# Router logits by feature blocks inside the last two column groups of an output projection, with a hand-written order and contiguous float16 parts

## The chip, the cores and the metric

The kernel runs on one core of a Trainium2 chip. Its metric is device time in microseconds, from one launch. The engines are TensorE (matrix products, transposes), VectorE, ScalarE, GpSimd (POOL) and SyncE (SP, which issues the loads). Each has its own queue and takes its instructions in the order of that queue; engines wait for each other by semaphores.

## The reference, cut to what matters

One block of a hybrid model for 512 tokens with 1024 features, in float32: gated mixing, cross attention, then a mixture of 32 experts in 4 groups, each added to the residual, and a last norm. The part that is touched is the end of the cross attention and the router:

```python
x = x + o.reshape(B, S, D) @ w_xo            # the residual, 512 x 1024
h = _rmsnorm(x, g_moe)                       # x * rsqrt(mean(x*x) + eps) * g
g_logits = h @ w_rg + b_rg                   # 4 groups
g_idx = argmax(g_logits)
e_logits = h @ w_re + b_re                   # 4 x 8 experts, those of the group g_idx count
top_v, top_i = top_k(e_sel, 2)               # two experts a token, softmax weights
for e in range(32):                          # only the chosen tokens have weight
    y += combine[:, e] * ((silu(h @ w_gate[e]) * (h @ w_up[e])) @ w_down[e])
```

Since the norm is one number per token and one gain per feature, the logits can be had from the raw residual: the gain goes into the router's weights beforehand, and the token's number is multiplied in afterwards.

## The kernel before, in words

Tokens stand in four blocks of 128 on the partitions; X1 (X2 inside `moe`) is the residual, block by block. Float32 products of the projections are made of three products of split operands (`mm3`, lines 98 to 101): the operand's high part, which ScalarE writes (line 121 for weights), and its low part, which VectorE writes (line 122).

`w_xo` is multiplied in four groups of 256 columns. The groups 0 and 1 are started inside the last head of the attention. Groups 2 and 3 follow: group 2 by halves of the features (`half`, 48 products each, 12 a block), group 3 block by block (`of_block`, 24 products), so that block 0 of the residual is ready first. The adds into the residual are line 522. `load_w` keeps three raw buffers and two pairs of split buffers; the numbers in `wx` give one load of this stage an extra raw buffer, and one an extra pair.

The router of a block is in `moe`: `turn` transposes the block's residual (line 755, eight transposes; columns are taken with a step of 8, as expert weights are laid out with eight consecutive features on a partition), ScalarE evacuates the first four (758) and VectorE the other four (760); line 762 squares and sums; the power -0.5 runs on POOL (95). `parts` scales the block and splits it into two float16 parts, the high one on ScalarE (771), the low one on VectorE (772). Both read the residual in order and write feature q*8+j to place j*128+q. `logits` is eight products of 40 columns (780). `choose` (786 to 810), for two blocks at once, picks group and experts with small VectorE instructions; `place` (812 to 831) counts, by products with a triangle of ones, which slot of its expert a token takes, and writes the selections of the first pair of experts (737, 738). `first` (875) gathers the first pair's tokens: products of the float16 parts with the selections. `numbers` (835 to 865) prepares each slot's token number (products of line 851) and the exponentials of the weights, and ends with a small Silu that brings its table in.

The experts go by pairs of two: gate and up products (1033, 64 a pair), transposes (1046), down products (1057), gathering for the next pair (1008, its copy 1010), combination (1083 to 1085). Weight pieces of 1 MB come in a ring of some fourteen buffers (922, 927) from a list in order of use; ten of the buffers have one size, and the router's transposes take one of those ten until its logits are done.

The order of work: a planner orders each engine's instructions by its own estimate of when they are ready, earlier-written work first. In a `manual_schedule` region the named engines keep the written order among the region's instructions; a region inside another adds its engines to those of the outer one, and the outer engines' order runs through it. Before, only TensorE has a written order: that of ROUT for the router, and that of the pairs for the experts. In ROUT a `w` is a block of group 3 (`w34` stands for four of its steps), T a turn, L logits, X parts, C choose, K place, G first, N numbers.

Of the kernel before, what the change touches and what calls it, by code (L numbers as in the profile page):

```python
# [9 lines left out]
F32 = mybir.dt.float32  # L10
# [10 lines left out]
P = 128  # L21
# [21 lines left out]
ROUT = "w0 w1 T0 w2 T1 w34 L0 T2 w3 L1 T3 C0 X0 X1 L2 L3 C1 K0 X2 X3 K1 G0 G1 N0 N1"  # L43
# [11 lines left out]
def emit(ctx, tc, a):  # L55
# [27 lines left out]
    colsv = consts.tile([P, 32], F32, name="colsv")  # L83
# [23 lines left out]
    def load_w(src, k0, nk, c0, n):  # L107
# [7 lines left out]
        if i == 3:  # L115
# [9 lines left out]
    def drain(g):  # L125
        for _ in g:
            pass
# [423 lines left out]
    rt_ = router_consts(ctx, nc, a, left, colsv[:, 24:32])  # L551
# [108 lines left out]
    rw = resid_rows(a["w_xo"], oth, otl, 2)  # L660
    drain(rw.half(0))
    drain(rw.half(4))
    rw.done()
    rw = resid_rows(a["w_xo"], oth, otl, 3)
    rw.loads()
    experts.load(NAHEAD)
    with tc.manual_schedule(engines={mybir.EngineType.PE}):
        fill = [rw.of_block(tb) for tb in range(NB)]

        def go(g, n=99):  # L670
            for _ in range(n):
                if next(g, "end") == "end":
                    return
        for w in ROUT.split():
            if w[0] == "w":
                go(fill[int(w[1])], int(w[2:] or 99))
            elif w[0] == "N":
                with tc.issue_after(router[-1].after_v):
                    router["N"](int(w[1]))
            else:  # L680
                router[w[0]](int(w[1]))
# [4 lines left out]
def router_consts(ctx, nc, a, left, gcol):  # L686
# [4 lines left out]
    c.gsc = rc.tile([P, KB], F32, name="gsc")  # L691
    V.tensor_scalar(c.gsc, gcol, 1.0 / XS, None, op0=OP.mult)
    c.wr = rc.tile([P, KB, NR], F32, name="wr")
    SP.dma_start(c.wr, a["w_r"])
    V.tensor_mul(c.wr, c.wr, c.gsc[:, :, None].to_broadcast([P, KB, NR]))
# [32 lines left out]
def moe(ctx, tc, a, X2, dram, small, acc, pss, pso, left, right, ident, rpow, wp, c, mraw):  # L728
# [16 lines left out]
    sq, lgs, m8s, ids = {}, {}, {}, {}  # L745

    def turn(tb):

        if not tTs:
            tTs.append(mraw.tile([P, 2, KB, P], F32, name="rsc", tag="mw", bufs=NRAW))  # L750
        tT = tTs[0][:, tb % 2]
        for j0 in range(0, KB, 4):
            pt = pss()
            for j in range(4):
                TE.transpose(pt[:, j * P:(j + 1) * P], X2[tb][:, j0 + j::KB], ident)
            ptv = pt.rearrange("p (j t) -> p j t", j=4)
            if j0 == 0:
                S.activation(tT[:, j0:j0 + 4], ptv, AF.Copy)
            else:
                V.tensor_copy(tT[:, j0:j0 + 4], ptv)  # L760
# [504 lines left out]
```

## Time and profile before

| | |
|---|---|
| median of three runs | 1316.55 us (1315.34 to 1319.72) |
| profiled execution | 1316.15 us, of it the span from first to last instruction 1314.4 us |
| TensorE busy | 1254.6 us, 95% of the span, mean granted clock 0.978 |
| VectorE, ScalarE, POOL busy | 561.8, 363.5, 128.9 us |
| loads | 278.45 MB, mean 212 GB/s, some 415 GB/s in the last third |

Times count from the first instruction. The projections with `w_xo` end, and the router runs, between some 730 and 815; the experts fill the rest. The granted clock is 1.0 where TensorE runs at 2.4 GHz and 0.5 at 1.2 GHz. A group of instructions has its line, engine and operation, output and input with their shapes, and its count. Busy time is a sum over instructions that may overlap.

### The profile page before, as it was taken

What the parts mean: (1) busy time and instruction counts of PE and PEld (TensorE: products, weight loads), DVE (VectorE), ACT (ScalarE), POOL (GpSimd) and SP (SyncE); (2) the same over time, 40 slices, a digit from 0 to 9 for tenths busy, and PEclk for the clock granted to TensorE, in tenths of its full rate; (3) what the DMA queues carried; (4) which work ended last, traced back from release to release, by engine and by line L of the source; (5) the groups of instructions that cost most, each with busy time, mean ns of one, the idle gap of its engine ahead of it and who ended that gap; (6) DMA issues with size and microseconds to landing.
All of it is one profiled execution on the core that took longest, in us unless ns stands there. A gap on an engine that the chain in (4) does not pass through costs nothing.

```text
span 1314.4 us, 18626 instructions
## 1 busy us (share of the span) xinstructions
PE 1254.6 (95%) x7606; PEld 903.1 (69%) x7606; DVE 561.8 (43%) x1050; ACT 363.5 (28%) x616; POOL 128.9 (10%) x250
## 2 busy tenths in 40 slices
PE   6999999999999999999999966999999999999996
PEld 5898998888888877899888965444444444444443
DVE  5346365234565645447455446132232322222225
ACT  5335343223344433336333253010000000000102
POOL 0002010000001100001000002111111221111001
PEclk9999999999999999999999976999999999999998
DMA  4343432344254335325411732899999999999971
GB/s 169 92 99 92 79 103 65 96 95 91 88 85 84 89 91 149 126 88 179 146 61 50 312 117 82 360 408 419 415 417 418 418 418 412 414 417 416 418 329 65
DMA packets 99113, 278.45 MB, mean 212 GB/s; under 512 B 6196, under 2 KB 67908, under 8 KB 77904
## 3 DMA queue, kind: packets, MB, share of 16 engines
q1 hardware_dynamic: 97536, 272.46, 57.8%
q0 software_dynamic: 1488, 4.76, 1.1%
q8 instruction: 61, 1.00, 0.3%
q14 instruction: 28, 0.23, 0.1%
HBM read 275.08 MB, written 2.12 MB: 211 GB/s over the span
## 4 chain that ended last, share of the span: by engine, by line
PE 90%; DVE 4%; ACT 3%; issue 1%; DMA 1%; POOL 0%; SPq 0%; POOLq 0%; ACTq 0%; DVEq 0%
PE acc L1033 18%; PE acc L99 16%; PE acc L101 16%; PE acc L100 16%; PE pso L1057 8%; PE pss L1008 4%; ACT xn L771 1%; PE pss L1083 1%; DVE xn L772 1%; PE pso L1084 1%; PE pso L1083 1%; PE pss L99 1%; PE pss L101 1%; PE pss L100 1%; PE pss L1046 1%
## 5 line engine op out<-in xcount | busy, mean ns | idle before, releaser
L1033 PE MATMUL acc<-mw,st 128*64 128x512 f32 x880 | 236.8, 599 | 0.0
L122 DVE TENSOR_TENSOR wl<-wraw,wh 128x1024 fp32r<-128x1024 f32 x120 | 146.9, 1225 | 186.0 <-ACT wh L121 181.5
L121 ACT ACTIVATE wh<-wraw 128x1024 fp32r<-128x1024 f32 x120 | 126.9, 1059 | 195.9 <-PE acc L100 91.1
L1033 PEld LDWEIGHTS acc<-mw,st 128*64 128x64 f32 x880 | 67.5, 137 | 108.2 <-issue 104.2
L99 PE MATMUL acc<-hH,wh 128*128 128x512 f32 x320 | 127.4, 398 | 0.0
L100 PE MATMUL acc<-hL,wh 128*128 128x512 f32 x320 | 126.8, 396 | 0.0
L101 PE MATMUL acc<-hH,wl 128*128 128x512 f32 x320 | 125.0, 398 | 1.7 <-DVE wl L122 1.7
L1068 DVE SCALAR_TENSOR_TENSOR yl<-pso,wsl,yh 128x512 fp32r<-128x512 f32 x32 | 22.6, 747 | 225.3 <-ACT yh L1067 225.3
L1057 PE MATMUL pso<-mw,hT 128*64 128x512 f32 x440 | 112.6, 592 | 0.7 <-ACT hT L1048 0.7
L100 PE MATMUL acc<-wl,hH 128*128 128x256 f32 x384 | 108.3, 282 | 1.1 <-DVE wl L122 1.1
L99 PE MATMUL acc<-wh,hH 128*128 128x256 f32 x384 | 108.2, 283 | 0.7 <-ACT wh L121 0.7
L101 PE MATMUL acc<-wh,hL 128*128 128x256 f32 x384 | 108.0, 282 | 0.2 <-DVE hL L193 0.2
L1019 POOL TENSOR_SCALAR G<-iot,code 128x64 f16<-128x64 f32 x120 | 49.8, 441 | 336.7 <-PE pss L1008 317.1
L1057 PEld LDWEIGHTS pso<-mw,hT 128*64 128x64 f32 x440 | 37.2, 137 | 61.4 <-issue 60.3
L100 PEld LDWEIGHTS acc<-wl,hH 128*128 128x128 f32 x384 | 72.7, 189 | 2.0 <-DVE wl L122 1.6
L99 PEld LDWEIGHTS acc<-wh,hH 128*128 128x128 f32 x384 | 72.7, 189 | 1.6 <-ACT wh L121 1.1
L101 PEld LDWEIGHTS acc<-wh,hL 128*128 128x128 f32 x384 | 72.6, 189 | 0.5 <-DVE hL L193 0.4
L1008 PEld LDWEIGHTS <-xn 128*128 128x128 f16 x960 | 55.0, 99 | 23.2 <-issue 22.7
L101 PEld LDWEIGHTS acc<-hH,wl 128*128 128x128 f32 x320 | 60.1, 188 | 15.8 <-DVE wl L122 2.2
L99 PEld LDWEIGHTS acc<-hH,wh 128*128 128x128 f32 x320 | 60.1, 188 | 13.2 <-ACT wh L121 0.4
L100 PEld LDWEIGHTS acc<-hL,wh 128*128 128x128 f32 x320 | 60.1, 188 | 13.2
L1067 ACT ACTIVATE yh<-pso,wsl 128x512 fp32r<-128x512 f32 x32 | 20.2, 683 | 154.3 <-PE pso L1057 154.3
(321 smaller groups left out, 2376.8 us busy)
## 6 DMA issues: line engine op xcount, KB each, us to landing
mw<-w_gate SPq DMA_DIRECT2D x55, 1024.0 KB, 12.6
mw<-w_up SPq DMA_DIRECT2D x55, 1024.0 KB, 11.7
mw<-w_down SPq DMA_DIRECT2D x55, 1024.0 KB, 10.2
wraw<-w_in SPq DMA_DIRECT2D x64, 512.0 KB, 5.4
wraw<-w_xkv SPq DMA_DIRECT2D x16, 512.0 KB, 3.4
mwl<-w_gate SPq DMA_DIRECT2D x10, 512.0 KB, 9.3
mwh<-w_up SPq DMA_DIRECT2D x10, 512.0 KB, 9.0
mwh<-w_down SPq DMA_DIRECT2D x10, 512.0 KB, 10.9
```

The source lines that it names most:

```text
L99: TE.matmul(out, ah, bh, start=start, stop=False, **kw)
L100: TE.matmul(out, ah, bl, start=False, stop=False, **kw)
L101: TE.matmul(out, al, bh, start=False, stop=stop, **kw)
L121: S.activation(h, raw, AF.Copy)
L122: V.tensor_sub(l, raw, h.bitcast(F32))
L1008: TE.matmul(pt[:, j * n:(j + 1) * n], c.XN[:, i % 2, i // 2, (4 * g + j) * P:(4 * g + j + 1) * P], G_[:, i // 2, :n], start=i == 0, stop=i ...
L1019: G.tensor_scalar(G_[:, tb, i * 64:i * 64 + 64], iot[:, :64], c.code[:, tb, e:e + 1], None, op0=OP.is_equal)
L1033: TE.matmul(ps[i][half(h)], sts[k // 4][:, k % 4, half(h)], w[i][k], start=k == 0, stop=k == KB - 1)
L1057: TE.matmul(o[n][half(h)], hT[:, j, half(h)], w[j][:, n * 512:(n + 1) * 512], start=j == 0, stop=j == 3)
L1067: S.activation(yh[:k, c], o[n][:k], AF.Copy, scale=wcol)
L1068: V.scalar_tensor_tensor(yl[:k, c], o[n][:k], wcol, yh[:k, c].bitcast(F32), op0=OP.mult, op1=OP.subtract)
L1083: TE.matmul(o, C[:k, ts], yh[:k, c], start=True, stop=False)
```

## The change

- The logits are taken in the natural order of features, by three stages of feature blocks: blocks 0 to 3 (columns 0 to 511), 4 and 5, 6 and 7. A stage is transposed and multiplied as soon as its columns of the residual stand: the first one among the products of group 2, the second among those of group 3, the last behind each block of group 3. All four blocks' logits gather in one PSUM bank. `w_r` and the gain come in a second layout for this.
- ROUT is a new list, and TensorE, VectorE and ScalarE all keep it. `a`, `b` are the halves of group 2 by block, `e` its adds, `v` the second load of group 3 and two more expert pieces, `t` and `l` a stage's transposes and logits of a block, `s` the squares of columns 0 to 767, `r` the rest of them and the power, `g` the scaling of the logits. Nine expert pieces are now written ahead of group 3's second load. The extra pair of split buffers goes to the third load in place of the fourth.
- `parts` reads the residual with a step of 8 elements (32 bytes) and writes its float16 output in order.
- `numbers` leaves ROUT. It is now called after the two stationary copies of the first pair, ahead of the first pair's products, with VectorE and ScalarE in written order too. The small Silu is gone.

```diff
@@ -40,7 +40,10 @@
 NAHEAD = 11
-ROUT = "w0 w1 T0 w2 T1 w34 L0 T2 w3 L1 T3 C0 X0 X1 L2 L3 C1 K0 X2 X3 K1 G0 G1 N0 N1"
+
+
+ROUT = ("a0 a1 t00 a2 t01 l00 a3 t02 l01 b0 t03 l02 v b1 l03 b2 b3 e s0 s1 w0 t10 t11 s2 w1 l10 l11 t12 t13 s3 r0 w2 l12 "
+        "l13 r1 t20 X0 w3 r2 t21 l20 g0 X1 r3 t22 l21 g1 C0 t23 l22 l23 K0 g2 g3 C1 X2 K1 X3 G0 G1")
 NR = 8 + NE
...
@@ -112,7 +115,7 @@
                      src[k0 * P:(k0 + nk) * P, c0:c0 + n].rearrange("(j p) n -> p j n", p=P))
-        if i == 3:
+        if i == 2:
             h = wx[1].tile([P, 1024], F32R, name="wh", tag="wraw", bufs=3)
...
@@ -657,28 +660,24 @@
     router, experts = moe(ctx, tc, a, X1, dram, small, acc, pss, pso, left, right, ident, rpow, wp, rt_, mraw)
-    rw = resid_rows(a["w_xo"], oth, otl, 2)
-    drain(rw.half(0))
-    drain(rw.half(4))
-    rw.done()
-    rw = resid_rows(a["w_xo"], oth, otl, 3)
-    rw.loads()
-    experts.load(NAHEAD)
-    with tc.manual_schedule(engines={mybir.EngineType.PE}):
-        fill = [rw.of_block(tb) for tb in range(NB)]
-
-        def go(g, n=99):
-            for _ in range(n):
-                if next(g, "end") == "end":
-                    return
+    rw2, rw3 = (resid_rows(a["w_xo"], oth, otl, c) for c in (2, 3))
+    with tc.manual_schedule(engines={mybir.EngineType.PE, mybir.EngineType.DVE, mybir.EngineType.Activation}):
+        rw2.loads()
+        rw3.ws = [rw3.load(0)]
+        experts.load(9)
         for w in ROUT.split():
-            if w[0] == "w":
-                go(fill[int(w[1])], int(w[2:] or 99))
-            elif w[0] == "N":
-                with tc.issue_after(router[-1].after_v):
-                    router["N"](int(w[1]))
+            n = [int(x) for x in w[1:]]
+            if w[0] in "ab":
+                drain(rw2.block(4 * "ab".index(w[0]), rw2.ws["ab".index(w[0])], n[0]))
+            elif w == "e":
+                rw2.done()
+            elif w == "v":
+                rw3.ws.append(rw3.load(4))
+                experts.load(NAHEAD)
+            elif w[0] == "w":
+                drain(rw3.of_block(n[0]))
             else:
-                router[w[0]](int(w[1]))
+                router[w[0]](*n)
     s_ot.close()
...
@@ -688,11 +687,13 @@
     rc = c.pool = ctx.enter_context(left("rc"))
-    c.gsc = rc.tile([P, KB], F32, name="gsc")
-    V.tensor_scalar(c.gsc, gcol, 1.0 / XS, None, op0=OP.mult)
+
+    gs2 = rc.tile([P, 2, KB], F32, name="gsc")
+    V.tensor_scalar(gs2, gcol.rearrange("p (a j) -> p a j", a=2), 1.0 / XS, None, op0=OP.mult)
+    c.gsc = gs2[:, 0]
     c.wr = rc.tile([P, KB, NR], F32, name="wr")
     SP.dma_start(c.wr, a["w_r"])
-    V.tensor_mul(c.wr, c.wr, c.gsc[:, :, None].to_broadcast([P, KB, NR]))
+    V.tensor_mul(c.wr, c.wr, gs2[:, 1, :, None].to_broadcast([P, KB, NR]))
     c.br = rc.tile([P, NR], F32, name="br")
...
@@ -743,42 +744,65 @@
     sq, lgs, m8s, ids = {}, {}, {}, {}
-
-    def turn(tb):
+    ss = rc.tile([P, NB, 2], F32, name="ss")
+
+    READY = ((0, 4), (4, 6), (6, 8))
+
+    def turned(stage, tb):
 
         if not tTs:
-            tTs.append(mraw.tile([P, 2, KB, P], F32, name="rsc", tag="mw", bufs=NRAW))
-        tT = tTs[0][:, tb % 2]
-        for j0 in range(0, KB, 4):
-            pt = pss()
-            for j in range(4):
-                TE.transpose(pt[:, j * P:(j + 1) * P], X2[tb][:, j0 + j::KB], ident)
-            ptv = pt.rearrange("p (j t) -> p j t", j=4)
-            if j0 == 0:
-                S.activation(tT[:, j0:j0 + 4], ptv, AF.Copy)
-            else:
-                V.tensor_copy(tT[:, j0:j0 + 4], ptv)
-        ss = small.tile([P, 1], F32, name="ss", tag="ss")
-        S.activation(c.XN[:, 0, tb].bitcast(BF), X2[tb], AF.Square, accum_out=ss)
+            tTs.append(mraw.tile([P, 4, 4, P], F32, name="rsc", tag="mw", bufs=NRAW))
+        k0, k1 = READY[stage]
+        if stage == 0:
+            return tTs[0][:, tb]
+        return tTs[0][:, 2 * stage - 2 + tb // 2, tb % 2 * 2:tb % 2 * 2 + 2]
+
+    def turn(stage, tb):
+        k0, k1 = READY[stage]
+        n = k1 - k0
+        pt = pss()
+        for j in range(n):
+            TE.transpose(pt[:, j * P:(j + 1) * P], X2[tb][:, (k0 + j) * P:(k0 + j + 1) * P], ident)
+        ptv = pt[:, :n * P].rearrange("p (j t) -> p j t", j=n)
+        if stage == 2:
+            V.tensor_copy(turned(stage, tb), ptv)
+        else:
+            S.activation(turned(stage, tb), ptv, AF.Copy)
+
+    lp = []
+
+    def logits(stage, tb):
+
+        if not lp:
+            lp.append(pso())
+        k0, k1 = READY[stage]
+        for k in range(k0, k1):
+            TE.matmul(lp[0][:, tb * NR:(tb + 1) * NR], turned(stage, tb)[:, k - k0], c.wr[:, k],
+                      start=k == 0 and tb == 0, stop=k == KB - 1 and tb == NB - 1, skip_group_check=True)
+
+    def squares(tb, cs=slice(0, 6 * P), i=0):
+        S.activation(c.XN[:, 0, tb, cs].bitcast(BF), X2[tb][:, cs], AF.Square, accum_out=ss[:, tb, i:i + 1])
+
+    def rstd(tb):
+        squares(tb, slice(6 * P, D), 1)
         v = small.tile([P, 1], F32, name="vv", tag="vv")
-        V.tensor_scalar(v, ss, 1.0 / (D * XS * XS), EPS / (XS * XS), op0=OP.mult, op1=OP.add)
+        V.tensor_scalar(v, ss[:, tb, 0:1], ss[:, tb, 1:2], D * EPS, op0=OP.add, op1=OP.add)
+        V.tensor_scalar(v, v, 1.0 / (D * XS * XS), None, op0=OP.mult)
         sq[tb] = rpow(v)
 
     def parts(tb):
 
-        xh, xl = (c.XN[:, i, tb].rearrange("p (j q) -> p q j", j=KB) for i in range(2))
-        xv = X2[tb].rearrange("p (q j) -> p q j", j=KB)
-        c.after_s = S.activation(xh, xv, AF.Copy, scale=sq[tb][:, 0:1]).ins
+        xh, xl = (c.XN[:, i, tb].rearrange("p (j q) -> p j q", j=KB) for i in range(2))
+        xv = X2[tb].rearrange("p (q j) -> p j q", j=KB)
+        S.activation(xh, xv, AF.Copy, scale=sq[tb][:, 0:1])
         V.scalar_tensor_tensor(xl, xv, sq[tb][:, 0:1], xh, op0=OP.mult, op1=OP.subtract)
 
-    def logits(tb):
+    def scaled(tb):
         h, i = tb // 2, tb % 2
         if i == 0:
             lgs[h] = rc.tile([P, 2, NR], F32, name="lg", tag="lg", bufs=2)
-        lp = pso()
-        for k in range(KB):
-            TE.matmul(lp[:, :NR], tTs[0][:, i, k], c.wr[:, k], start=k == 0, stop=k == KB - 1)
-        V.scalar_tensor_tensor(lgs[h][:, i], lp[:, :NR], sq[tb][:, 0:1], c.br, op0=OP.mult, op1=OP.add)
+        V.scalar_tensor_tensor(lgs[h][:, i], lp[0][:, tb * NR:(tb + 1) * NR], sq[tb][:, 0:1], c.br,
+                               op0=OP.mult, op1=OP.add)
 
...
@@ -853,12 +877,9 @@
             ge = rc.tile([P, NG], F32, name="ge", tag="ge", bufs=1)
-            gl_ = S.activation(ge, lgs[h][:, i, :NG], AF.Exp, bias=ngm[:, 0:1], accum_out=c.gs[:, tb:tb + 1])
-            last = S.activation(c.dv[:, tb:tb + 1], m8s[h][:, i, 1, 1:2], AF.Exp, bias=ngm[:, 1:2])
+            S.activation(ge, lgs[h][:, i, :NG], AF.Exp, bias=ngm[:, 0:1], accum_out=c.gs[:, tb:tb + 1])
+            S.activation(c.dv[:, tb:tb + 1], m8s[h][:, i, 1, 1:2], AF.Exp, bias=ngm[:, 1:2])
         if h:
-            warm = small.tile([P, 1], F32, name="warm", tag="warm")
-            with tc.issue_after(gl_.ins), tc.issue_after(last.ins):
-                S.activation(warm, c.gs[:, 0:1], AF.Silu)
 
...
@@ -875,9 +896,8 @@
 
-    router = dict(G=first, T=turn, X=parts, L=logits, C=choose, K=place, N=numbers)
-    router[-1] = c
-
+    router = dict(G=first, X=parts, C=choose, K=place, t=turn, l=logits, s=squares, r=rstd, g=scaled)
+    c.numbers = numbers
     experts = Experts(ctx, tc, a, X2, dram, small, acc, pss, pso, left, right, ident, rpow, wp, c, mraw)
...
@@ -1092,7 +1112,10 @@
     with tc.manual_schedule(engines={mybir.EngineType.PE}):
-        sts = [stationary(c.G0, g, pt=c.pts[g]) for g in range(2)]
+        with tc.manual_schedule(engines={mybir.EngineType.DVE, mybir.EngineType.Activation}):
+            sts = [stationary(c.G0, g, pt=c.pts[g]) for g in range(2)]
+            for h in range(2):
+                c.numbers(h)
         before = None
...
@@ -1243,11 +1266,12 @@
         "w_gates": wg.reshape(KB, P, 36).transpose(1, 0, 2), "gbias": gb,
-        "vecs": np.concatenate([col(g_ml_head), col(b_gate_ml), col(b_gate_fx), f(g_moe).reshape(P, KB)], axis=1),
+        "vecs": np.concatenate([col(g_ml_head), col(b_gate_ml), col(b_gate_fx), f(g_moe).reshape(P, KB),
+                                col(g_moe)], axis=1),
         "w_proj_ml": f(w_proj_ml)[0], "w_proj_fx": f(w_proj_fx)[0], "w_out": f(w_out)[0],
         "g_xq": f(g_xq), "g_xmem": f(g_xmem), "w_xq": f(w_xq)[0], "w_xkv": f(w_xkv)[0],
         "w_xo": f(w_xo)[0],
-        "w_r": wr.reshape(P, KB, NR),
+        "w_r": wr.reshape(KB, P, NR).transpose(1, 0, 2),
         "b_r": np.concatenate([f(b_rg), np.full((1, 8 - NG), -3.0e38, np.float32), f(b_re)], axis=1),
```

## Rows read from the trace of the kernel before

**Rows 1.** Busy time by stretch: length, each engine's busy time, granted clock, DMA share, GB/s.
```profile
787.00:809.00 22.00, 9.99 (x51) 9.67 (x51) 17.00 (x57) 9.99 (x22) 0.56 (x1) 0.50 0.34 131
...
826.90:831.00 4.10, 1.65 (x13) 0.90 (x13) 1.81 (x7) 0.00 (x0) 0.00 (x0) 1.00 1.02 430
831.00:834.20 3.20, 3.20 (x34) 3.00 (x33) 1.01 (x6) 0.00 (x0) 0.00 (x0) 0.51 1.00 417
...
920.00:1000.00 80.00, 79.18 (x474) 35.84 (x473) 23.92 (x37) 6.11 (x10) 14.54 (x27) 1.00 1.01 416
```

**Rows 2.** What SP's queue waited for, 728 to 1310: total us, times, longest.
```profile
SPq L922 <- PE acc L1033: 234.1, 52, 17.4
```

**Rows 3.** The chain that ended last: shares of 755 to 835; then pieces.
```profile
by line: ACT xn L771 24.5%; DVE xn L772 19.8%; PE acc L1033 15.8%; PE pss L875 7.3%; issue 5.1%; PE pss L1008 4.0%; ACT xn L762 2.9%; POOL rpow L95 2.8%; DVE rsc L760 2.4%; DVE Vw L972 2.4%; PE pss L974 2.1%; PE acc L101 1.0%; PE acc L100 1
...
809.39 5.84 PE pss L875 x64
815.32 7.01 PE acc L1033 x30
...
839.83 3.58 PE acc L1033 x16
```

**Rows 4.** Instruction groups by shape, ScalarE and VectorE: count, busy us, mean ns, idle before.
```profile
L771 ACT ACTIVATE xn<-x,rpow 128x1024 f16<-128x1024 f32 x4 | 19.6, 4896 | 10.4 <-POOL rpow L95 10.4
L762 ACT ACTIVATE xn<-x 128x1024 bf16<-128x1024 f32 x4 | 4.2, 1051 | 13.2 <-DVE x L522 13.2
...
L772 DVE SCALAR_TENSOR_TENSOR xn<-x,rpow,xn 128x1024 f16<-128x1024 f32 x4 | 19.1, 4774 | 17.2 <-ACT xn L771 17.2
L215 DVE SCALAR_TENSOR_TENSOR xn<-x,rpow,gxq 128x1024 f32<-128x1024 f32 x4 | 5.1, 1286 | 0.7 <-POOL rpow L95 0.7
L824 DVE TENSOR_REDUCE rk<-jk 128x4 f32<-128x128 f32 x2 | 0.6, 283 | 0.0
L800 DVE TENSOR_REDUCE es<-ex 128x16 f32<-128x64 f32 x2 | 0.5, 260 | 0.0
```

**Rows 5.** VectorE in order of time, adds of `w_xo`: start, duration, instruction.
```profile
743.22 0.69 DVE L522 TENSOR_TENSOR x<-x,acc 128x512 f32<-128x512 f32 x1 [2.15 <-PE acc L101]
...
757.42 0.42 DVE L522 TENSOR_TENSOR x<-x,acc 128x256 f32<-128x256 f32 x1 [2.16 <-PE acc L101]
```

**Rows 6.** TensorE in order of time, sixteen logit products.
```profile
773.40 1.87 PE L780 MATMUL pso<-wr,rsc 128*128 128x40 f32 x16
```

**Rows 7.** VectorE in order of time, choice, placing and slot numbers.
```profile
793.69 0.16 DVE L789 MAX8 m<-lg 128x8 f32<-128x8 f32 x1
...
795.54 0.27 DVE L800 TENSOR_REDUCE es<-ex 128x16 f32<-128x64 f32 x1
...
803.79 0.40 DVE L802 MAX8 m<-es 128x8 f32<-128x8 f32 x2
...
805.52 0.17 DVE L810 TENSOR_TENSOR ab<-eb 128x64 bf16<-128x64 bf16 x1
...
809.42 0.29 DVE L822 TENSOR_TENSOR jk<-eb,pso 128x128 f32<-128x128 bf16 x1
...
811.23 0.61 DVE L738 SCALAR_TENSOR_TENSOR G<-iot,cd,GA 128x128 f16<-128x128 f32 x2
811.75 0.16 DVE L839 TENSOR_SCALAR rf<-rk 128x4 f32<-128x4 f32 x1
...
814.37 0.69 DVE L1010 TENSOR_TENSOR st<-pss,gsc 128x512 f32<-128x512 f32 x1
...
815.87 0.38 DVE L849 TENSOR_SCALAR Vj<-eb,tokn 128x64 f16<-128x64 bf16 x2
```

**Rows 8.** SP's queue in order of time: the fourth load of `w_xo`, expert pieces.
```profile
731.10 0.37 SPq L113 DMA_DIRECT2D wraw<-w_xo  x1
...
734.93 2.65 SPq L922 DMA_DIRECT2D mw<-w_gate  x2
```

**Rows 9.** Loads issued from 728 to 760: count, KB each, median us to landing.
```profile
mw<-w_gate SPq DMA_DIRECT2D x5, 1024.0 KB, 17.0
```

More of the change, by code (lines that the diff above doesn't have):

```diff
@@ L82, in emit @@
     make_identity(nc, ident)
-    colsv = consts.tile([P, 32], F32, name="colsv")
+    colsv = consts.tile([P, 40], F32, name="colsv")
     gbias = consts.tile([36, 1], F32, name="gbias")
@@ L550, in emit @@
     s_mg.close()
-    rt_ = router_consts(ctx, nc, a, left, colsv[:, 24:32])
+    rt_ = router_consts(ctx, nc, a, left, colsv[:, 24:40])
     s_ot = ExitStack()
@@ L830, in place @@
         for tb in (2 * h, 2 * h + 1):
-            c.after_v = c.hits(c.G0, c.GA, cd[:, tb % 2], tb)
+            hits(c.G0, c.GA, cd[:, tb % 2], tb)
     def numbers(h):
```

## The prediction

> **What bounds the kernel now.** I read the table of stretches first, then the chain of waits, then the two queues that matter. In the long stretch of experts TensorE is busy 79.18 of 80 us at full clock, with the DMA share at 1.01 [rows 1]; SP waits there for TensorE to give buffers back (234.1 us in 52 waits) [rows 2], so TensorE sets the pace and every microsecond by which the first expert product starts earlier comes off the end. That product starts at about 815.3 [rows 3]. The stretch before it is the opposite: between 787 and 809 TensorE works 9.99 of 22 us, at clock 0.50 [rows 1]. The chain names the cause: of 755 to 835, 24.5% is line 771 on ScalarE and 19.8% line 772 on VectorE [rows 3], the two halves of the float16 parts. Each runs 4 times, 4.896 and 4.774 us [rows 4]. The same number of elements costs ScalarE 1.051 us (line 762) and VectorE 1.286 us (line 215) where reads and writes are contiguous [rows 4]. They sit in front of everything else on their engines: a block's evacuation, sum of squares and choice wait behind the parts of the block before.
>
> **Front of the new order.** The second halves of w_xo's first two groups are done when the add at 743.22 may start [rows 5]: I count TensorE from 743.0. From there to the add at 757.42 stand five blocks of 24 products, 2.86 us each [rows 5], and the two last groups have eight: 22.9. Up to the end of w3 the order puts 26 transposes and 24 logits between them, 50 at 1.87/16 = 0.117 [rows 6], 5.9 us: w3 ends at 771.8. Nothing here waits long: evacuations run on ScalarE while the next block multiplies, the squares of six feature blocks lie beside w0 to w2, and the conversions of three of the four loads have had their turn. The power on POOL is asked for early by r0 and r1. Before, part of these transposes and logits ran at half clock, between 787 and 809 [rows 1].
>
> **Tail of the new order.** Now VectorE is the queue that counts, since its order is fixed. Counted from row pairs, first and last of a part:
> - one half's choice (13 kinds of small instruction): 793.69 to 795.81 is 2.1 for the first part, less 0.7 in which a copy stood between; 803.79 to 805.69 is 1.9 for the second part with other work between [rows 7]. I take 3.2, between 2.8 and 3.6.
> - one half's placing: 809.42 to 811.84, 2.4 [rows 7].
> - the slot numbers of both halves: 811.75 to 816.25, less 2 x 0.62 for the two stationary copies among them, 3.25 [rows 7].
> - the low part, one block: X, below 1.9.
> VectorE ends the low part of block 0 at about 772.5 and then does: w3's add (0.42 at line 522 [rows 5]), block 2's variance, an evacuation, a scaled logit, none of them wider than that, 1.5; low part of block 1 1.9; variance, evacuation, logit 1.0; first choice 3.2; evacuation 0.4; a trip over TensorE for logits and counts 0.8; first placing 2.4; two logits 0.5; second choice 3.2; low part of block 2 1.9 (it hides the second trip); second placing 2.4; low part of block 3 1.9. That is 21.1, so 793.6. The last gathering products on TensorE, half of the 64 that took 5.84 at half clock [rows 3], lie mostly beside the second placing and the last low part; 0.4 stays before the first stationary copy (0.69 [rows 7]), 0.8 before the second (0.69).
>
> **The wait that is added.** The slot-number products were free to fall behind the first expert products, and did. Now they stand in TensorE's fixed order ahead of them, and their VectorE work stands in its fixed order behind both stationary copies. So the first expert product waits 3.25 + 0.3 more. Behind it on TensorE waits everything. Sum: 793.6 + 0.4 + 0.69 + 0.8 + 0.69 + 3.25 + 0.3 = 799.7. After that wait TensorE starts cold: the gap of 826.9 to 831.0 (1.65 busy of 4.10) was followed by 3.2 us at clock 0.51 [rows 1]. In the old order the gathering products carried the slow start. I add 2.0 (bounds 0 and 3): 801.7 in place of 815.25. The gain is 13.5 us.
>
> **X, the price of the parts.** Before, they read contiguously and wrote 2-byte elements 256 bytes apart; after, they write contiguously and read 4-byte elements 32 bytes apart. No row shows that on ScalarE. Bounds: 1.05 and 1.29 if the stride costs nothing, 4.90 and 4.77 if it costs what the written one did [rows 4]. The nearest row is line 800, a VectorE sum whose inner step is 32 bytes: 0.260 us for 64 elements, where line 824 takes 0.283 for 128 in order [rows 4]. In order an element costs 1.12 ns (1.286 less 0.283, over 896), so 0.14 is fixed, and the step of 32 bytes costs 1.9 ns an element, 1.9 us for 1024. I take 1.9 for both engines. ScalarE's share is off the chain up to about 2.5 us, as it has little else after 767. With X at the lower bound the first product starts 2.0 earlier; at the upper one 14.7 later.
>
> The Trainium skill speaks against this edit (Advanced Engine Details and Errata, section Memory Cachelines): accesses that stay in one 16-byte line of SBUF run at full speed, and a different line at every access pays a penalty; 32 bytes is a new line each time, on the read side as 256 was on the write side. Line 800 agrees that there is a penalty and puts it at under one half of the written one's. Taken as one price for reads and writes, the rule gives the third rival.
>
> **Queues and what costs nothing.** SP's order stays with the planner. The fourth w_xo load went out at 731.10, ahead of nine expert pieces, the last of them at about 737.2 [rows 8]. It is now emitted behind them. Pieces issued then landed 17.0 us later in the median [rows 9]; so behind eight or nine of them this load lands at 755 to 761 instead of 735, its conversion holds ScalarE and VectorE's queues (behind it s0 and the two adds of "e", then the transposes of stage 1), and w0's second half waits. I work out 0.8 for landing at 758 and 3.8 for 761. I take 0: the planner freed that load's buffer first before, too. The remaining pieces go into buffers that come free at w3 and at the last logits, 772 and 781, some 18 us ahead of the first expert product. The Silu table, loaded by the removed warm-up, is now loaded at the first use, 1.3 us; that lies beside the 16 products (3.58 us [rows 3]) that stand ahead of the consumer, and costs 1.3 if it does not. POOL's selections for the second pair start when the codes are there, as before. Splitting the squares adds four instructions to ScalarE before the tail; the 40-column constant and the second layout of w_r are nothing beside a queue that idles there.
>
> **Rivals.** (1) The stride is nearly free and the clock rises during the gathering products: start at 797.8, gain 17.5, 1298.7. For it: contiguous writes; against: line 800. (2) The fourth load is late: 803.6 + 2.0, gain 9.7, 1306.5. For it: it is emitted behind the pieces; against: its buffer frees early. (3) Strided reads cost what strided writes cost: 814.4 + 2.0, a loss of 1.1, 1317.3, no change within what can be told. For it: both engines paid nearly the same 4.8 us, so memory set it, not the engine; against: line 800. (4) The other side: the strided read is dearer than the strided write. Four low parts and the wait for the first high part stand on the fixed queue, so each further microsecond of X on both engines costs 5. From X = 5.5 on the kernel is slower; at twice the old price (9.7 and 9.6) the start is 838.4 + 2.0, 25 later, 1341. For it: four-byte reads move twice the bytes; against: line 800 again, which would have to be 0.5 us long for X = 5.5.
>
> **Numbers.** The profiled execution took 1316.15 us, 1.75 more than its span and 0.4 under the median of 1316.55. 1316.15 - 13.5 = 1302.7. Chances: forecast 0.55 (its own range, from X of 1.4 to 2.6, the clock's 0 to 3 and a choice of 2.8 to 3.6, is 1298 to 1308), rival 1 0.18, rival 2 0.13, rival 3 0.09, rival 4 0.05. A measurement here tells about 0.3%, 4 us, from no change. Faster: 0.55 + 0.18 + 0.13 = 0.86; the same 0.09; slower 0.05. The range of 8 in 10 goes from 1296 to 1313, which leaves out the last two rivals and the rim of the first.
>
> **What would show it.** In the profile after: line forms of the two parts near 1.9 us; VectorE nearly gapless from 772 to 799, TensorE sparse and at half clock there; the slot products ahead of the first expert product, which starts near 800; several microseconds at half clock behind it; SP's fourth w_xo load ahead of or behind the pieces; the pace of the later pairs unchanged. The forecast falls if the parts cost over 4 us, if TensorE starves for w_xo before w0, or if an expert pair becomes longer.

## The result, and the profile after

The changed kernel takes 1307.99 us (median of 4 runs, 1307.27 to 1310.08) against 1316.38 for the kernel before beside it: a ratio of 0.9935, interval 0.9913 to 0.9956. It is faster, by 8.4 us and not by the 13.5 that were forecast. A second series of the same kernel gave 1308.02.

I cut every profiled execution at two marks: the start of the last add of column groups 0 and 1 (at 743.22 before [rows 5]), which stands just ahead of the first thing that the change moves, and the start of the first expert product (815.25 before). The front ends at the first mark, the router's stretch lies between the two, and the rest are the experts. The table also has the kernels of the experiments.

| kernel | median, us | ratio to before | add starts | router | experts | span |
|---|---|---|---|---|---|---|
| before | 1316.4 to 1317.0 | 1 | 743.22 | 72.0 | 499.2 | 1314.4 |
| changed | 1307.99 | 0.9935 | 748.04 | 58.2 | 502.1 | 1308.3 |
| again | 1308.02 | 0.9928 | 748.17 | 58.2 | 499.4 | 1305.8 |
| parts_only | 1297.19 | 0.9849 | 743.66 | 52.5 | 498.9 | 1295.1 |
| order_only | 1323.37 | 1.0041 | 748.01 | 72.4 | 501.9 | 1322.3 |
| late_numbers | 1303.46 | 0.9897 | 747.91 | 53.8 | 497.5 | 1299.2 |
| shifted | 1301.21 | 0.9882 | 746.72 | 52.6 | 500.0 | 1299.3 |
| shift64 | 1298.34 | 0.9856 | 743.86 | 52.5 | 500.0 | 1296.4 |
| consts_apart | 1305.58 | 0.9911 | 745.63 | 58.2 | 502.0 | 1305.9 |
| after48 | 1305.90 | 0.9910 | 744.38 | 58.1 | 501.7 | 1304.2 |
| free_order | 1310.11 | 0.9951 | 748.25 | 60.4 | 501.5 | 1310.1 |
| combined | 1299.91 | 0.9875 | 744.33 | 54.7 | 499.2 | 1298.2 |

So the router gave back 13.8 us, the front took 4.8 away before the change had even begun, and the experts took 0.3 to 2.9. The profiled execution of the changed kernel was its longest one (1310.08). The six times of consts_apart lie in two groups (1302.4 to 1303.6, 1307.6 to 1307.9), those of free_order too (1308.2 to 1308.4, 1311.8 to 1314.4), and both profiles are of the upper group, so that these two medians say little.

The busy time of the changed kernel by stretch (columns as in rows 1):
```profile
748.00:777.60 29.60, 29.52 (x256) 29.29 (x255) 7.89 (x14) 13.19 (x25) 1.46 (x3) 1.00 0.57 225
777.60:806.20 28.60, 11.86 (x118) 10.64 (x116) 25.60 (x97) 11.46 (x24) 3.94 (x8) 0.75 0.45 165
...
806.20:809.50 3.30, 3.30 (x10) 1.02 (x11) 0.34 (x2) 0.00 (x0) 3.30 (x9) 0.50 0.02 5
...
920.00:1000.00 80.00, 79.22 (x474) 35.27 (x474) 20.74 (x32) 6.64 (x11) 14.60 (x27) 1.00 1.01 415
```
Read the third and the first column of times together. Up to 777.6 TensorE has no gap and VectorE works 7.9 of 29.6 us. From there it is the other way round: VectorE 25.6 of 28.6, TensorE 11.9. The router now has two bounds, one behind the other. The first expert products run at clock 0.50. The pace of the later pairs is that of before [rows 1].

The two parts in the changed kernel, grouped by shape, ScalarE first (columns as in rows 4, where they took 4.896 and 4.774):
```profile
L797 ACT ACTIVATE xn<-x,rpow 128x1024 f16<-128x1024 f32 x4 | 8.9, 2220 | 1.8 <-POOL rpow L98 1.8
...
L798 DVE SCALAR_TENSOR_TENSOR xn<-x,rpow,xn 128x1024 f16<-128x1024 f32 x4 | 8.4, 2105 | 0.8 <-ACT xn L797 0.8
```

VectorE of the changed kernel in order of time: start, duration, line, and what ended its idle time. The first row is the first mark; then come the four low parts, the two stationary copies and the last of the slot numbers.
```profile
748.04 0.69 DVE L525 TENSOR_TENSOR x<-x,acc 128x512 f32<-128x512 f32 x1 [2.13 <-PE acc L104]
...
777.61 2.25 DVE L798 SCALAR_TENSOR_TENSOR xn<-x,rpow,xn 128x1024 f16<-128x1024 f32 x1 [0.82 <-ACT xn L797]
...
780.92 2.07 DVE L798 SCALAR_TENSOR_TENSOR xn<-x,rpow,xn 128x1024 f16<-128x1024 f32 x1
...
794.15 2.06 DVE L798 SCALAR_TENSOR_TENSOR xn<-x,rpow,xn 128x1024 f16<-128x1024 f32 x1
...
798.60 2.05 DVE L798 SCALAR_TENSOR_TENSOR xn<-x,rpow,xn 128x1024 f16<-128x1024 f32 x1
...
801.13 0.69 DVE L1030 TENSOR_TENSOR st<-pss,gsc 128x512 f32<-128x512 f32 x1 [0.33 <-PE pss L896]
802.03 0.69 DVE L1030 TENSOR_TENSOR st<-pss,gsc 128x512 f32<-128x512 f32 x1 [0.20 <-PE pss L896]
...
805.62 0.43 DVE L873 TENSOR_SCALAR Vj<-eb,tokn 128x64 f16<-128x64 bf16 x2
```

TensorE of the changed kernel, in order of time: transposes and logits of four feature blocks for one token block, the end of its last block of w_xo, and the way into the experts.
```profile
752.52 0.60 PE L765 MATMUL pss<-ident,x 128*128 128x128 f32 x4
752.96 0.98 PE L780 MATMUL pso<-wr,rsc 128*128 128x40 f32 x8
...
778.89 0.28 PE L104 MATMUL acc<-wh,otl 128*128 128x256 f32 x1
...
800.70 1.29 PE L896 MATMUL pss<-G,xn 128*128 128x128 f16 x20 [1.58 <-DVE xn L798]
804.25 0.35 PE L875 MATMUL acc<-Vj,R 128*128 128x32 f16 x4 [2.26 <-DVE Vj L873]
805.96 0.36 PE L875 MATMUL acc<-Vj,R 128*128 128x32 f16 x4 [1.36 <-DVE Vj L873]
806.25 13.43 PE L1053 MATMUL acc<-mw,st 128*64 128x512 f32 x48
```
Two things are to be seen. A token block's first stage is four logit products, and the trace has eight instructions for it. And the last gathering product ends at about 802, but the first expert product starts at 806.25, behind eight small slot-number products, each set of four waiting for VectorE.

### The profile page after: what moved, and what is told of

Its sections match the earlier page's. It is cut to its first block, busy times and chain, and to the rows that moved or that the text cites. A ratio compares the mean times of both kernels' runs of the same rounds, so it can differ in the third digit from the quotient of the medians.

```text
span 1308.3 us, 18639 instructions
## 1 busy us (share of the span) xinstructions
PE 1253.9 (96%) x7606; PEld 899.9 (69%) x7606; DVE 552.9 (42%) x1054; ACT 355.4 (27%) x627; POOL 130.0 (10%) x250
## 3 DMA queue, kind: packets, MB, share of 16 engines
q1 hardware_dynamic: 97536, 272.46, 58.1%
## 4 chain that ended last, share of the span: by engine, by line
PE 92%; DVE 4%; ACT 1%; issue 1%; DMA 1%; POOL 0%; SPq 0%; POOLq 0%; ACTq 0%; DVEq 0%
PE acc L1053 18%; PE acc L102 16%; PE acc L104 16%; PE acc L103 16%; PE pso L1077 8%; PE pss L1028 4%; PE pss L1103 1%; PE pso L1103 1%; PE pso L1104 1%; PE pss L102 1%; PE pss L104 1%; PE pss L103 1%; PE pss L1066 1%; PE pss L1104 1%; DVE st L1030 1%
## 5 line engine op out<-in xcount | busy, mean ns | idle before, releaser
L1053 PE MATMUL acc<-mw,st 128*64 128x512 f32 x880 | 239.5, 608 | 0.0
L103 PEld LDWEIGHTS acc<-hL,wh 128*128 128x128 f32 x320 | 60.7, 190 | 13.4
```

The costliest lines, as they stand in the source:

```text
L103: TE.matmul(out, ah, bl, start=False, stop=False, **kw)
L1053: TE.matmul(ps[i][half(h)], sts[k // 4][:, k % 4, half(h)], w[i][k], start=k == 0, stop=k == KB - 1)
```

## The experiments

**again**: the changed kernel a second time, no edit.

> The changed kernel, unaltered, for a second profile. In the first one the stage ahead of the router ended 4.8 us later than before (an add at 748.04 in place of 743.22), although all engines take the same instructions there. If that is the spread of single executions, this profile shows the add within 1.5 us of 743.2 and the median stays near 1308. If it belongs to the program (addresses have moved by the eight added columns of constants), the add is again at 747 to 749.

Measured: 1308.02 us (1305.99 to 1308.56), the add at 748.17, the router 58.2. The later front is no accident of one execution. The experts took 499.4 us instead of 502.1: the 48 products of the first pair took 11.8 us up to the first weights' product at 818.19, in place of 13.4. What the clock costs there varies from run to run: over the first 3.3 us of the experts it is 0.57 in this profile and 0.50 in the first.

**parts_only**: the kernel before, with nothing but the two contiguous parts.
```diff
-        xh, xl = (c.XN[:, i, tb].rearrange("p (j q) -> p q j", j=KB) for i in range(2))
-        xv = X2[tb].rearrange("p (q j) -> p q j", j=KB)
+        xh, xl = (c.XN[:, i, tb].rearrange("p (j q) -> p j q", j=KB) for i in range(2))
+        xv = X2[tb].rearrange("p (q j) -> p j q", j=KB)
```

> The kernel before with one edit: the float16 parts read with the step and write in order. Theory A (the fixed order of VectorE's queue and the stages by feature blocks carry the gain, cheaper parts are a share of it): each part falls from 4.8 to about 2.1 us as in the changed kernel, the chain through four blocks keeps its other links, and the gain is some 5 us or less, 1311 or more. Theory B (the parts alone are the gain): four blocks follow each other 5.4 us sooner each, 1295 to 1303, so the rest of the change gives nothing or costs.

Measured: 1297.19 us (1295.82 to 1298.46), ratio 0.9849 (0.9835 to 0.9862): better than both kernels, by 20 and 11 us. In the router the order of instructions on each engine is that of the kernel before. Its parts by shape, over the router's stretch:
```profile
L771 ACT ACTIVATE xn<-x,rpow 128x1024 f16<-128x1024 f32 x4 | 8.9, 2236 | 5.2 <-POOL rpow L95 5.2
...
L772 DVE SCALAR_TENSOR_TENSOR xn<-x,rpow,xn 128x1024 f16<-128x1024 f32 x4 | 8.5, 2129 | 6.6 <-ACT xn L771 6.6
```
The same kernel in order of time: first mark, first high part, first expert product.
```profile
743.66 0.69 DVE L522 TENSOR_TENSOR x<-x,acc 128x512 f32<-128x512 f32 x1 [2.15 <-PE acc L101]
...
760.32 2.29 ACT L771 ACTIVATE xn<-x,rpow 128x1024 f16<-128x1024 f32 x1 [0.85 <-POOL rpow L95]
...
796.18 7.08 PE L1033 MATMUL acc<-mw,st 128*64 128x512 f32 x30 [0.20 <-DVE st L1010]
```
And its busy time by stretch:
```profile
743.60:771.00 27.40, 25.76 (x217) 25.31 (x215) 11.23 (x14) 10.89 (x12) 1.10 (x2) 1.00 0.67 263
771.00:796.10 25.10, 18.40 (x150) 18.00 (x150) 18.66 (x90) 10.65 (x24) 2.38 (x5) 0.66 0.44 166
...
796.10:799.40 3.30, 3.22 (x16) 1.20 (x18) 1.07 (x5) 0.00 (x0) 3.30 (x9) 1.00 0.02 5
```
The first high part starts 16.7 us after the mark; in the changed kernel it starts 27.3 after it. ScalarE there, the last evacuation of stage 1, the squares of block 0's last 256 columns, and the high part:
```profile
772.31 0.66 ACT L770 ACTIVATE rsc<-pss 128x256 f32<-128x256 f32 x2 [2.98 <-PE pss L765]
...
773.68 0.42 ACT L784 ACTIVATE xn<-x 128x256 bf16<-128x256 f32 x1
...
775.29 2.29 ACT L797 ACTIVATE xn<-x,rpow 128x1024 f16<-128x1024 f32 x1 [0.70 <-POOL rpow L98]
```
Block 0's last add starts at 767.57 there, 19.5 us after the mark, where it starts 14.2 after it here: TensorE does transposes and logits first. The other half of the delay is ScalarE's written order: the squares stand behind the evacuations of stage 1, which wait for TensorE, and start 6.1 us after that add (0.5 here). VectorE's work is spread over both halves of the stretch (11.2 and 18.7 us), where the new order leaves 25.6 for the end. And the first expert products run at full clock.

**order_only**: the changed kernel with the parts as before (the edit above, backwards).

> The changed kernel with the parts as before (they read in order and write with the step). Theory A: the order still gains, 1310 to 1314. Theory B, by the sum of the prediction with 4.9 and 4.8 in place of the measured 2.2 and 2.1: the tail on VectorE grows by 13 us and the time is 1319 to 1323, slower than before.

Measured: 1323.37 us (1320.25 to 1324.01), ratio 1.0041 (1.0028 to 1.0055): slower than before, by 0.4%. The parts by shape, over the router's stretch:
```profile
L797 ACT ACTIVATE xn<-x,rpow 128x1024 f16<-128x1024 f32 x4 | 19.6, 4908 | 1.7 <-POOL rpow L98 1.7
...
L798 DVE SCALAR_TENSOR_TENSOR xn<-x,rpow,xn 128x1024 f16<-128x1024 f32 x4 | 19.3, 4820 | 3.5 <-ACT xn L797 3.5
```
Its router takes 72.4 us where that of the kernel before took 72.0. Stages, early logits, the written order and the wait for the slot numbers, all together, gain nothing there; the front loses 4.8 and the experts 2.7 (their first product again stands behind the slot numbers). 4.8 + 0.4 + 2.7 is the 7.9 by which the span grew. No run takes that wait away beside the dear parts, so what the stages alone do there is not shown. The router is 14.2 us longer than in the changed kernel; the prediction's third rival, with the same price of the parts, had 14.7.

**late_numbers**: the changed kernel, but the first 32 expert products are issued ahead of the slot-number products.
```diff
+            ps0 = [acc(), acc()]
+            gu0 = gate_up(sts, [(ex.rows(e, 0), ex.rows(e, 1)) for e in (0, 1)], ps0)
+            advance(gu0, 8)
...
-            ps = [acc(), acc()]
-            gu = gate_up(sts, [(ex.rows(e, 0), ex.rows(e, 1)) for e in es], ps)
+            if p == 0:
+                ps, gu = ps0, gu0
...
-            advance(gu, 4)
+            advance(gu, 4 if p else 0)
...
```
The first lines stand between the stationary copies and the slot numbers.

> The changed kernel with the slot-number products behind the first 32 expert products of the first pair; VectorE's and ScalarE's order is kept. If the wait for them is a cost of its own, as the prediction has it, the first expert product starts 3.3 us sooner and the cold start shrinks by up to 1 us: 1303.5 to 1305. If the wait was covered by the cold clock or by the stop at the weights' sums behind it, the time stays at 1307 to 1308.

Measured: 1303.46 us (1301.0 to 1303.94), 4.5 less than the changed kernel. TensorE in order of time:
```profile
800.53 1.29 PE L896 MATMUL pss<-G,xn 128*128 128x128 f16 x20 [1.58 <-DVE xn L798]
801.75 7.09 PE L1053 MATMUL acc<-mw,st 128*64 128x512 f32 x32
808.78 0.26 PE L875 MATMUL acc<-Vj,R 128*128 128x32 f16 x4
```
The router is 4.4 us shorter. The granted clock of the first expert products, by stretch, in this kernel:
```profile
801.70:805.00 3.30, 3.30 (x19) 1.21 (x18) 3.00 (x11) 0.00 (x0) 1.57 (x4) 1.00 0.02 5
```
Without the pause between gathering and experts the clock is 1.00, where it was 0.50: nineteen products in 3.3 us instead of ten.

**shifted**: parts_only with its first constants tile eight columns wider, as the change made it. The columns are never used; all later tiles of that side lie 32 bytes higher.
```diff
-    colsv = consts.tile([P, 32], F32, name="colsv")
+    colsv = consts.tile([P, 40], F32, name="colsv")
...
-        SP.dma_start(colsv, a["vecs"])
+        SP.dma_start(colsv[:, 0:32], a["vecs"])
```

> The kernel with only the parts changed (1297.2), and the tile of constants that is allocated first widened from 32 to 40 columns, the added eight never used: what lies behind it moves by 32 bytes, as in the changed kernel. Four profiles of the changed kernel and its variants ended the stage ahead of the router 4.3 to 5 us later (add at 748 in place of 743.2 and 743.7) with the same instructions. Theory A (the moved addresses cost it): add at 747 to 749, 1300.5 to 1302. Rival (something else in the changed program, its loads at the start or the order of a few products): add at 743 to 744.5, 1297 to 1298.

Measured: 1301.21 us (1300.64 to 1301.65), 4.0 more than parts_only, all of it ahead of the router or varying in the experts; the router is the same 52.6.

**shift64**: the same with a tile of 48 columns, so that the tiles lie 64 bytes higher.

> The kernel before with the parts in order, and its first constants tile 48 columns wide instead of 32 (the 16 more are never used): all later tiles of that side lie 64 bytes higher, where 8 columns more (32 bytes) gave 1301.2 against 1297.2. Theory A, what costs is that later tiles no longer begin on a multiple of 64 bytes: about 1297, and TensorE's pace between 50 and 500 us as in the kernel before (drift under 0.5 us). Theory B, any move costs, by where tiles fall against each other: about 1301, with a drift near 3 us.

Measured: 1298.34 us (1295.35 to 1299.17), and the add at 743.86. Apart from the columns that the load fills, the three kernels differ in one number, the width of that tile. They were measured in three series; the kernel before read 1317.03, 1316.51 and 1316.57 beside them. Two ScalarE instructions of each in order of time, an evacuation near 43 and a conversion near 497; first parts_only:
```profile
43.35 0.60 ACT L349 ACTIVATE th<-acc 128x512 f32<-128x512 f32 x1 [1.77 <-PE acc L101]
...
496.93 2.01 ACT L121 ACTIVATE wh<-wraw 128x1024 fp32r<-128x1024 f32 x2 [5.24 <-PE acc L100]
```
shifted by 32 bytes:
```profile
44.55 0.60 ACT L349 ACTIVATE th<-acc 128x512 f32<-128x512 f32 x1 [1.82 <-PE acc L101]
...
500.81 2.01 ACT L121 ACTIVATE wh<-wraw 128x1024 fp32r<-128x1024 f32 x2 [5.26 <-PE acc L100]
```
shifted by 64 bytes:
```profile
43.45 0.60 ACT L349 ACTIVATE th<-acc 128x512 f32<-128x512 f32 x1 [1.82 <-PE acc L101]
...
497.26 2.01 ACT L121 ACTIVATE wh<-wraw 128x1024 fp32r<-128x1024 f32 x2 [5.22 <-PE acc L100]
```
The same work took 453.6, 456.3 and 453.8 us. TensorE is busy nearly throughout (over 453 of the 454 us from 43 to 497 in each), so it is its pace that fell, by 0.6%, with 32 bytes and not with 64. The profiles of all twelve kernels agree: the six with tiles 32 bytes higher need 456.3 to 456.6 us between these two instructions, the six with 0 or 64 bytes 453.5 to 454.1.

**consts_apart**: the changed kernel with the constants tile at 32 columns again; the second layout of the gain is loaded into the router's own tile.
```diff
-    colsv = consts.tile([P, 40], F32, name="colsv")
+    colsv = consts.tile([P, 32], F32, name="colsv")
...
+    SP.dma_start(gs2[:, 1], a["vecs"][:, 32:40])
```

> The changed kernel with its first tile of constants at 32 columns as before; the second layout of the gain is loaded into the router's own tile. Theory A (moved addresses): the stage ahead of the router ends at 743 to 744.5 and the time is 1302.5 to 1304.5. Rival: 748 and 1308.

Measured: 1305.58 us (1302.4 to 1307.93), 2.4 less. In its profile the front is 2.4 us longer than before all the same: 1.2 in the first 45 us and 1.5 at some 505 us, in two single steps (0.3 came back later); between them it did not drift. What makes the first step is open. The second is TensorE's clock. Its busy time around 505, in the kernel before and in this one:
```profile
499.00:509.00 10.00, 8.44 (x36) 6.86 (x37) 8.08 (x11) 3.15 (x6) 0.00 (x0) 1.00 0.60 116
```
```profile
500.00:510.00 10.00, 8.27 (x30) 6.58 (x30) 7.87 (x11) 3.19 (x5) 0.00 (x0) 0.83 0.56 111
```
In both, TensorE had just waited 1.73 us for VectorE. Then it ran on at full clock in the kernel before; here the next products, some eight, go at half clock, one every 0.43 us in place of 0.23. The changed kernel, again and order_only have the same 0.83 there, the other eight 1.00.

**after48**: the changed kernel with a tile of 48 columns in place of 40, eight of them unused.

> The changed kernel with its first constants tile 48 columns wide instead of 40 (8 unused). Theory A: the 32-byte offset goes, so 1304.5 to 1305.5, as where the layout was loaded into a tile of its own (1305.6), with a drift under 0.5 us up to 500 us. Theory B: 1308 as the changed kernel.

Measured: 1305.90 us (1301.71 to 1306.46), 2.1 less than the changed kernel and 0.4 above the range of theory A; the drift is 0.5. VectorE at the first mark and TensorE at the second:
```profile
744.38 0.69 DVE L525 TENSOR_TENSOR x<-x,acc 128x512 f32<-128x512 f32 x1 [2.13 <-PE acc L104]
...
802.48 13.24 PE L1053 MATMUL acc<-mw,st 128*64 128x512 f32 x48
```
The first expert product is 3.8 us earlier than at 806.25, by the front alone: by the pace, and by the step of clock near 505, which this profile has not. The medians show 2.1 of it; the difference lies within what the experts vary.

**free_order**: the changed kernel with only TensorE's order fixed in the router, so that the planner orders VectorE and ScalarE.
```diff
-    with tc.manual_schedule(engines={mybir.EngineType.PE, mybir.EngineType.DVE, mybir.EngineType.Activation}):
+    with tc.manual_schedule(engines={mybir.EngineType.PE}):
```

> The changed kernel with only TensorE's order written out in the router's list; VectorE and ScalarE are left to the planner there, which lets the two halves' choices and placings and the low parts of blocks 2 and 3 run between each other. Theory A (the written order of VectorE's queue costs, since small dependent instructions stand one behind the other): the tail shrinks by 2 to 5 us, 1303 to 1306. Rival (VectorE has the same work in either order): 1307 to 1309. If the planner puts the adds or evacuations late: over 1309.

Measured: 1310.11 us (1308.15 to 1314.35); the router takes 60.4 us, 2.2 more. This is the third case of the expectation. The planner sets the add of block 2 behind a low part, and TensorE's last block of w_xo waits for it; its first product:
```profile
780.32 0.58 PE L102 MATMUL acc<-wh,oth 128*128 128x256 f32 x1 [3.72 <-DVE x L525]
```
Its products then follow at half clock, one every 0.21 us in place of 0.12. Block 0's high part does start 5.3 us sooner (22.0 after the mark). So the planner's order is no better than the written one, and whether the written order costs against parts_only stays open: a better order of VectorE and ScalarE was not tried.

**combined**: consts_apart, late_numbers and free_order together.

> The changed kernel with three mends at once: constants at their old width, slot-number products behind the first 32 expert products, VectorE and ScalarE left to the planner in the router. If the three costs are separate (4.5, 4.5 and 2 to 5 us) they add up to 1294 to 1297, about the kernel with the parts alone (1297.2); a sum that falls short by over 2 us would say that two of them hide each other.

Measured: 1299.91 us (1299.8 to 1300.84), the router 54.7. That is 2.9 above the upper end of the sum: two costs of 4.5 account for it, and the planner's order gave nothing. With the offset and the wait gone, the stages are still 2.2 us behind parts_only in the router and 2.7 in the median (of another series); late_numbers, in the written order, is 1.3 behind it in the router (53.8 against 52.5). The contiguous parts alone remain the best version.

## Why the prediction was right in direction and 5.3 us short

The forecast's own range was 1298 to 1308, and the time lies at its rim. It is nearer to the 1306.5 of the second rival than to the 1302.7 of the forecast, but that is chance: what that rival says did not happen (the late load, below). Step by step, in the profiled executions; the moments after 743 are shifted by the 4.8 us of the front:

- **The price of the parts, X = 1.9: right in kind, 0.2 to 0.3 low.** 2.22 and 2.11 us. The working left out its own fixed part: 0.14 and 1024 elements at 1.9 ns are 2.06. All three rivals on the price fell with this: "nearly free", "strided reads cost what strided writes cost" and "dearer". The 2.0 us for the lower bound was wrong too: four low parts shorter by 0.6 are 2.4, and more with ScalarE's. The Trainium skill (Advanced Engine Details and Errata, section Memory Cachelines) puts a penalty on going to a different line at each access. The trace agrees that there is one: VectorE's 2.11 stands against 1.286 in order [rows 4]. The trace's strided read takes under one half of its strided write (2.11 against 4.77).
- **TensorE's front, w3 at 771.8: 2.4 us short.** With the 4.8 it should have ended at 776.6; the last product starts at 778.89. I counted 24 logits as 24 instructions of 0.117. The row that I priced them from says 16 for the eight logit products of one token block [rows 6]: each product is two instructions. The trace after has eight per stage of four, 0.81 us from the first to what follows. So 48 at 0.10 are 4.9 where the sum has 2.8: 2.1 of the 2.4, and the rest is spread over small steps. The blocks of w_xo were taken at 2.86; the row gives 2.84, 0.2 less in all. Since TensorE has no gap there, the 2.4 go onto the path: the last low part ends 2.2 later than worked out.
- **VectorE's tail, 21.1 us: right.** From the end of block 0's low part (777.61 + 2.25 = 779.86) to that of block 3's (798.60 + 2.05 = 800.65) it is 20.8. The table of stretches shows it nearly gapless, as said (25.6 of 28.6 us). TensorE is sparse there, as said too, but at a mean clock of 0.75 and not at half.
- **Stationary copies and slot numbers, 6.1: 5.6.** The added wait was real: late_numbers takes it away, and the router shrinks by 4.4 (0.9 above the 3.55 put down). Up to the first expert product the whole chain was forecast at 56.5 us from the mark and took 58.2.
- **The cold clock, 2.0: right in kind.** 0.50 behind the wait, 1.00 without it. The first pair lost 1.7 us against parts_only (13.4 for 48 products against 11.65) in the profile of the changed kernel and 0.2 in its second one.
- **The late fourth load: no.** SP's queue in the changed kernel, in order of time, the last two loads of w_xo and the first expert piece:
```profile
729.90 6.48 SPq L116 DMA_DIRECT2D wraw<-w_xo  x2
736.48 0.46 SPq L942 DMA_DIRECT2D mw<-w_gate  x1
```
All loads of w_xo go ahead of the expert pieces. The Silu table, on ScalarE:
```profile
794.44 1.28 ACT L1059 ACT_TABLE_LOAD   x1
```
It is loaded with ScalarE idle, 11.8 us ahead of the first expert product, and costs nothing.
- **The step that failed: "the 40-column constant and the second layout of w_r are nothing beside a queue that idles there".** I asked what the eight columns cost to load, not what lies behind them. They moved the later tiles by 32 bytes, and the front, which the change does not touch, ended 4.8 us later. Some 3 of these are the offset: shifted against shift64 gives 2.9, both in the median and at the first mark, and between the instructions near 43 and 497 the changed kernel takes 456.5 us where the kernel before takes 453.6. The rest are single steps. 1.3 us fall into the first 43 us, and their cause is open. Near 505 a stretch at half clock costs 1.6 (see consts_apart). Near 657 it is the other way round; the kernel before, then the changed one:
```profile
654.00:666.00 12.00, 10.07 (x49) 8.44 (x49) 5.60 (x16) 2.81 (x9) 0.00 (x0) 0.86 0.13 45
```
```profile
658.00:670.00 12.00, 10.09 (x56) 8.35 (x56) 5.67 (x15) 3.24 (x8) 0.00 (x0) 1.00 0.26 86
```
That gives 1.5 back, so the two steps of clock nearly cancel here; in after48's 3.7 at the first mark the one near 505 is in.

The account closes: 4.8 + (58.2 - 56.5) + (2.9 - 2.0) = 7.4 is the difference between the forecast 13.5 and the 6.1 by which the profiled span shrank. By the medians the gain is 8.4.

What the forecast did not ask at all is how the gain divides. It took the change as one, and the gain came from two lines of it; that the direction held is due to them. The parts are worth 19.5 us in the router by themselves (72.0 to 52.5). All the rest adds nothing: with the dear parts the router is 72.4 against 72.0, with the cheap ones 58.2 against 52.5. Of these 5.7 the wait for the slot numbers is 4.4 (late_numbers), so the stages and the written order cost 1.3 beside the cheap parts. Beside the dear ones they may gain what the wait costs there; no run shows it.

Why they gain nothing beside the cheap parts is read from the tables and not tried by itself. They move TensorE's logits ahead, but the high part of block 0 then starts 10.6 us later than in parts_only, half of it behind TensorE's extra work and half behind ScalarE's written order. Then the choice, the placing and the parts pile up on VectorE. A start 5.3 us sooner was not enough: free_order has it and loses it again to a late add and the clock.

## What to carry to other kernels

Before a change of many parts is built, price each by itself on the path: here the two lines that made the writes contiguous were worth more than the whole. TensorE work that is moved ahead of a chain that VectorE ends should let VectorE start earlier too; here it started later (a reading of the tables, as said). Count instructions from the row that gives the duration, not from the source. And where a constants tile grows, look at the pace of stages that the change does not touch: here 32 bytes more cost 3 us, and 64 bytes nothing that could be told.

## What was not expected of the hardware

- Moving the tiles by 32 bytes slowed TensorE's matrix products by 2.7 us in 453.6 us (0.6%), seen in the profiles of all six kernels with that shift and in none of the six with a shift of 0 or 64 bytes. Which operand does it, and whether other offsets do, was not tried.
- A read of 4-byte elements at steps of 32 bytes with writes in order took 2.1 us for 1024 elements on each of 128 partitions on VectorE and 2.2 on ScalarE; the write of 2-byte elements at steps of 256 bytes took 4.8 and 4.9 [rows 4].
- Some 4 us in which TensorE does only eight small products, between gathering and experts, bring the next 3.3 us to a granted clock of 0.50 (0.57 in the second profile of the same kernel); where the expert products follow the gathering at once, it is 1.00.
- The same wait of TensorE, 1.72 or 1.73 us near 500, was followed by some eight products at half clock in four kernels (a granted clock of 0.83 over 10 us) and by none in the other eight (1.00). That is worth 1.5 us.
